# Four small tiles padded: where the tiles of a five-stage transformer program start in SBUF

## The chip, the cores and the metric

The program runs on one core of one Trainium2 chip. The metric is the device time in microseconds of one execution, the median of several runs. The trace is one profiled execution of the same program.

## The reference, cut to what matters

512 tokens of width 1024 pass through two blocks of two layers each. Everything is float32.

```python
for l in range(2):      # first block
    h = rms_norm(x, norm_mix_pre[l])
    proj = h @ w_in[l]                                  # 1024 x 2560
    o_da, o_ret, o_pool = ...   # two-map attention, retention, windowed means
    mix = concatenate([o_da, o_ret, o_pool]) @ w_out[l]
    x = x + rms_norm(mix, norm_mix_post[l])
    h = rms_norm(x, norm_mlp_pre[l])
    u = h @ w_up[l]                                     # 1024 x 5632
    uc = conv_b + sum(conv_w[j] * shifted(u, j) for j in range(3))
    gate, val = split(uc)
    x = x + rms_norm((gelu(gate) * val) @ w_down[l], norm_mlp_post[l])
for l in range(2):      # second block
    x = x + 0.5 * swiglu(rms_norm_2(x), gate, up, down) # inner width 2816
    x = x + hybrid_mixer(rms_norm_2(x))                 # dilated windows, stick breaking, gates
    x = x + 0.5 * swiglu(rms_norm_2(x), gate, up, down)
out = rms_norm_2(x, norm_final)
```

## The kernel before

Ten stages run one after the other: mix1, mlp1, mix1, mlp1 (the first block), then ffn1, mix2, ffn2 twice (the second). In each of them PE does the dense products, and smaller work (attention, retention, pooling, stick breaking) is put between them in program order. That order is fixed when the program is built: every triple of dense matmuls adds a nominal 640 ns to a clock in the program's text (tick, called at the end of each triple), and a generator of small work takes its next step when its credit is positive. No measured time enters into it.

**Weights.** Class Stream loads weights in chunks of 128 x 1024 float32 (tile wraw, DMA from the SP queue), then ACT copies each to whi in float32r (L63), and DVE subtracts to get wlo (L64), so that whi + wlo is the weight. There are 3 wraw and 4 pairs of whi and wlo. Activations are split in the same way: h_hi and h_lo, hid_hi and hid_lo, mix, fm, od and os. A product of two split numbers takes three float32r matmuls: high by high, and the two cross terms.

**Dense products.** Two forms exist. In the feature-major one (fm, fm_block, mm3a: L166, L167, L168) 128 x 128 blocks of the weights are stationary and 512 tokens of h move, eight blocks deep, into a PSUM bank called pa; mix2's two projections use the same three lines with od and os moving, into pp. The opening four chunks of a stage run by halves, 256 tokens each, so that they can begin while the last tokens' norm is still under way. In the token-major form (tm, mm3b: L172, L173, L174) 128 tokens of an activation are stationary and 512 columns (256 for mix2's values) of the weights move, into pb. The activation there is h (mix1's first two products, mix2's values), hid (the down products of mlp1, ffn1 and ffn2), mix (mix1's output) or the split gates fm_hi and fm_lo (mix2's output). For two of mix2's three groups of values the stationary tokens are every fourth one.

**Stage ends.** finish adds the last product to X, squares and scales X for the next norm (xn, L199), and PE transposes the rows (L209) into the next h; the chain of those steps is placed beside the first half matmuls of the next stage.

**Layout.** Tiles lie in pools, in the order in which the pools were opened: const, keep, small, gains, sq, wraw, wparts, then a pool for each stage (phase). A tile takes the bytes of its row in each partition, rounded up to a multiple of 32. const holds ident (512 bytes), mhalf (32 bytes) and X, keep holds h_hi and h_lo, small holds the norms' and the mixers' small tiles and xn. Behind mhalf, X, h_hi, h_lo and xn therefore start 32 bytes past a multiple of 128. gains, wraw, whi, wlo and the stage pools start on a multiple of 128, since what lies in small adds up that way. In mlp1's pool cw (528 bytes, 544 with rounding) and cb (176, 192 with rounding) stand ahead of hid_hi, so hid_hi and hid_lo start at 96 modulo 128; ffn1 and ffn2 use the same function without cw and cb, and hid starts at 0. In mix1's pool cols, share and lam (32, 160 and 32 bytes) put v_da, vg, u, the masks, the tiles fm and the pairs mix_hi, mix_lo at 96. In mix2's pool all tiles start at 0.

Of the kernel before, what the change touches and what calls it, by code (L numbers as in the profile page):

```python
# [11 lines left out]
F32 = mybir.dt.float32  # L12
# [6 lines left out]
L = 2  # L19
D = 1024  # L20
T = 512
NT = T // 128
KD = D // 128
FF = 2816
KF = FF // 128
# [12 lines left out]
class Stream:  # L38
    """Weights in the order of their use: each chunk is loaded, split in two
    float32r parts whose sum it is, and given out."""  # L40

# [42 lines left out]
class Background:  # L84
    """Work that is spread between the dense products: generators, each of which
    yields how much dense work (in ns) it wants before its next step."""

# [4 lines left out]
class Block:  # L92
# [16 lines left out]

# [1 line left out]

# [29 lines left out]

# [1 line left out]

# [31 lines left out]

# [1 line left out]

# [16 lines left out]
    def scaled_rows(self, t, r, gain):  # L194
        """Rows of block t of the norm's output, in two halves."""
        parts = []
        for n in range(2):
            xn = self.small.tile([128, 512], F32, name="xn", bufs=4)
            self.nc.vector.scalar_tensor_tensor(xn, self.X[:, t, n * 512:(n + 1) * 512], r,  # L199
                                                gain[:, n * 512:(n + 1) * 512], op0=OP.mult, op1=OP.mult)  # L200
            parts.append(xn)
        return parts
# [11 lines left out]
    def later(self, ns, t, f):  # L214
        """f, which works on token block t, after so much more dense work."""
        self.pending.append((self.clock + ns, t, f))
        self.pending.sort(key=lambda x: x[0])

    def flush(self, t):
        """Whatever is still to do for the token blocks up to t."""  # L220
        while True:
            i = next((i for i, x in enumerate(self.pending) if x[1] <= t), None)
            if i is None:
                return
            self.pending.pop(i)[2]()

# [1 line left out]

    def fm(self, evacs, halves=False):
        """Feature-major products: one chunk [128, 8, 128] for each of evacs."""  # L230
        tag = self.dense_tag
        blocks = []
        n = self.n_half if halves else 0
        if halves and n < len(evacs):
            self.fm(evacs[:n], True)
            return self.fm(evacs[n:])
        groups = [evacs] if halves else [[e] for e in evacs]
        for group in groups:
            got = []
            for e in group:  # L240
                if not halves:
                    got.append((self.st.take(), self.bank(tag, "pa"), e))
            if halves:
                for h in range(2):
                    self.flush(2 * h + 1)
                    for j, e in enumerate(group):
                        if h == 0:
                            got.append((self.st.take(), self.bank(tag, "pa"), e))
                        (i, w), ps, _ = got[j]
                        c = slice(h * 256, (h + 1) * 256)  # L250
                        self.fm_block(ps, w, c, 256)
                        if h == 1:
                            self.st.release(i)
                            got[j][2](ps)
            else:
                for (i, w), ps, e in got:
                    self.fm_block(ps, w, slice(0, 512), 512)
                    e(ps)
                    self.st.release(i)
# [7 lines left out]
    def tm(self, nk, width, rows, evac, tag, tail=0, opens=False):  # L267
        """Token-major products: nk feature blocks against chunks of CHUNK // width
        blocks of width columns each."""
        per = CHUNK // width  # L270
# [35 lines left out]

# [1 line left out]

    def finish(self, nk, rows, gain, scale=None, post=None, final=False):
        """x += the product of rows with the next weights (scaled, or normed with  # L310
        the gain post), then the next norm's rows on their way to self.H."""
        nc = self.nc
# [62 lines left out]
    def begin(self, gain):  # L375
        """The first norm, in the order in which tokens and weights arrive."""
        nc = self.nc
# [39 lines left out]

# [1 line left out]

# [43 lines left out]
    def mlp1(self, l, next_gain, final):  # L463
        nc, a = self.nc, self.a
        cw = self.phase.tile([128, 3, 2 * KF], F32, name="cw")
        cb = self.phase.tile([128, 2 * KF], F32, name="cb")
        nc.sync.dma_start(cw, a["conv_w"][l])
        nc.sync.dma_start(cb, a["conv_b"][l])
        post = a["norm_mlp_post"][l]
        self.mlp((cw, cb), next_gain, final, post)  # L470
# [3 lines left out]

# [1 line left out]

# [3 lines left out]
    def spare(self, name):  # L480
        """A scratch tile from the slots that the norms use between the stages."""
        return self.small.tile([128, 512], F32, name=name, tag="xn", bufs=4)
# [28 lines left out]

# [1 line left out]

    def mix1(self, l, next_gain, final):
# [10 lines left out]
        load(lams, bass.AP(tensor=s.tensor, offset=s.offset, ap=[[0, 128], [64, 4], [1, 64]]))  # L525
        cols = ph.tile([128, 8], F32, name="cols")
        load(cols, a["mix_cols"][l])
# [80 lines left out]
    def diff_attention(self, fm, v, neglam, gcol, mix):  # L608
# [4 lines left out]
        def scores(h, t):  # L613
            n = 128 * (t + 1)
            q, k = fm[f"q{h}"], fm[f"k{h}"]
            if t == 0:
                rec[h] = self.small.tile([128, NT, 2], F32, name="rec", bufs=3)
            st = self.small.tile([128, 8], F32, name="st")
# [92 lines left out]
    def retention(self, fm, vg, gcols, mix):  # L711
        """The decay of a query and the inverse decay of a key are in their rotary
        tables, so a block's past is one state per head."""
        nc = self.nc
# [74 lines left out]
    def pooling(self, u, share, pw, gcols, mix):  # L789
        """Means over windows of 2 and 4, then 8 and 16 tokens, by halves."""  # L790
        nc = self.nc
# [27 lines left out]

# [1 line left out]

# [101 lines left out]
    @staticmethod  # L923
    def tokens(x, g, t):
        """The tokens of tile t of group g, of x [p, T]: a run of tokens, or the
        tokens that are t modulo 4, one or four whole residue classes."""
        return x[:, t::4] if g else x[:, t * 128:(t + 1) * 128]

    def dilated(self, half, fm, v, o_dil):
# [4 lines left out]
        for s in range(2):  # L934
# [6 lines left out]
            def near(i):  # L941
                """Scores of key blocks 2i and 2i + 1, each for its own and the next block."""
                ps = self.bank(self.bg_tag, "pst")
                for b in (2 * i, 2 * i + 1):
                    n = min(256, T - b * 128)
                    mm(ps[:, (b % 2) * 256:(b % 2) * 256 + n], k[0][:, b * 128:(b + 1) * 128], q[0][:, b * 128:b * 128 + n])
                x = self.scratch("es")
                if i == 0:
                    f = lambda a: a.rearrange("p (a b) -> p a b", a=2)
                    nc.vector.tensor_add(f(x), f(ps), pair)  # L950
                else:
                    nc.vector.tensor_add(x[:, :384], ps[:, :384], self.window_kq3)
                return x
# [49 lines left out]
            yield 900  # L1003
            # weights, numerators and denominators
            mt = m.rearrange("p (i t) -> p t i", t=4)
# [95 lines left out]
def body(ctx, tc, a, out, stages):  # L1101
# [5 lines left out]
    nc.sync.dma_start(B.ident, a["c_ident"])  # L1107
    B.mhalf = B.const.tile([128, 8], F32, name="mhalf")
    nc.vector.memset(B.mhalf, -0.5)
# [13 lines left out]
def constants():  # L1123
    """Tables that depend on the shapes alone."""
    c = {}
# [39 lines left out]
def tiles_a(w):  # L1165
    """[L, D, N] as chunks [L, N // 128, 128, 8 * 128] of whole columns."""
    n = w.shape[2] // 128
    return w.reshape(L, KD, 128, n, 128).transpose(0, 3, 2, 1, 4).reshape(L, n, 128, CHUNK)


def tiles_b(w, width):
    """[L, K, N] as chunks [L, (N // width) * (K // 128 // per), 128, per * width]."""
    per = CHUNK // width
# [4 lines left out]
def arrange(inp):  # L1178
    """The inputs laid out as the program reads them."""
    a = {}  # L1180
# [61 lines left out]
```

## Time and profile before

| | |
|---|---|
| median of 3 runs | 3564.27 us (3563.7 to 3566.45) |
| span of the profiled execution | 3553.4 us |
| PE busy | 3500.0 us, 98% |
| PE weight loads | 2842.4 us, 80% |
| DVE, ACT, POOL busy | 1512.6, 1163.3, 351.3 us |
| DMA | 312 MB, mean 88 GB/s |

The profiled execution's own time is its span of 3553.4 us and what lies around it at the start and the end; the median is 10.9 us above the span. A line of the profile names the program's line, the engine, the operation, out<-in by the tiles' names with buffer numbers left out, the shape and a count. PE's matmuls are pipelined, so their durations overlap: the time that one costs is the distance between two starts.

### The profile page before, as it was taken

How to read it: one execution, taken by the hardware profiler on the slowest of the kernel's cores; microseconds unless marked ns; L12 is line 12 of the kernel's file. 1: busy time of each engine (PE TensorE's matmuls, PEld its weight loads, DVE VectorE, ACT ScalarE, POOL GpSimd, SP SyncE). 2: the span in 40 equal slices, each digit the busy share in tenths (PEclk: the TensorE clock that was granted, in tenths of full speed). 3: DMA queues.
4: the chain of work that ended last, by engine and by line, in shares of the span. 5: the costliest groups of instructions: out<-in, count | busy, mean ns of one | idle time of the engine just before them, and what ended most of it. 6: DMA issues, size and time to landing. Idle time of an engine off the chain costs nothing.

```text
span 3553.4 us, 39868 instructions
## 1 busy us (share of the span) xinstructions
PE 3500.0 (98%) x16304; PEld 2842.4 (80%) x16304; DVE 1512.6 (43%) x1973; ACT 1163.3 (33%) x1854; POOL 351.3 (10%) x412
## 2 busy tenths in 40 slices
PE   8999999999999999999999999999999999999999
PEld 6678887767888788889887888888888988788887
DVE  4655542465554343324543533233332454353322
ACT  4344432334443232222235332222222223532222
POOL 2411100241110000002200100000000220010000
PEclk9999999999999999999999999999999999999999
DMA  4123232312223232222111232323222211123232
GB/s 154 47 73 101 95 107 78 110 48 73 100 95 108 76 102 94 101 101 88 49 60 60 89 102 94 104 86 101 94 100 97 88 48 60 61 90 104 92 104 77
DMA packets 87191, 312.00 MB, mean 88 GB/s; under 512 B 10369, under 2 KB 11073, under 8 KB 87009
## 3 DMA queue, kind: packets, MB, share of 16 engines
q1 hardware_dynamic: 85536, 305.17, 25.3%
q0 software_dynamic: 1472, 4.30, 0.4%
q8 instruction: 128, 2.10, 0.2%
q14 instruction: 55, 0.44, 0.0%
HBM read 307.32 MB, written 2.10 MB: 87 GB/s over the span
## 4 chain that ended last, share of the span: by engine, by line
PE 93%; DVE 3%; ACT 1%; POOL 1%; issue 1%; DMA 0%; DVEq 0%; SPq 0%; POOLq 0%; ACTq 0%
PE pa L166 19%; PE pa L167 18%; PE pa L168 18%; PE pb L172 10%; PE pb L173 10%; PE pb L174 10%; PE pst L932 1%; PE pz L1038 1%; PE psc L625 1%; DVE wlo L64 1%; PE ph L209 1%; PE pod L1026 1%; PE pos L1038 1%; PE po L661 1%; DVE pb L343 0%
## 5 line engine op out<-in xcount | busy, mean ns | idle before, releaser
L64 DVE TENSOR_TENSOR wlo<-wraw,whi 128x1024 fp32r<-128x1024 f32 x556 | 708.5, 1277 | 1207.0 <-ACT whi L63 1205.7
L166 PE MATMUL pa<-h_hi,whi 128*128 128x512 f32 (+1 forms) x3072 | 1180.7, 384 | 4.4 <-ACT h_hi L151 4.4
L167 PE MATMUL pa<-h_lo,whi 128*128 128x512 f32 (+1 forms) x3072 | 1158.6, 377 | 5.7 <-DVE h_lo L152 5.7
L168 PE MATMUL pa<-h_hi,wlo 128*128 128x512 f32 (+1 forms) x3072 | 1157.5, 377 | 0.0
L63 ACT ACTIVATE whi<-wraw 128x1024 fp32r<-128x1024 f32 x556 | 583.3, 1052 | 685.4 <-PE pb L174 516.8
L166 PEld LDWEIGHTS pa<-h_hi,whi 128*128 128x128 f32 x3072 | 578.5, 188 | 136.5 <-issue 16.0
L168 PEld LDWEIGHTS pa<-h_hi,wlo 128*128 128x128 f32 x3072 | 578.3, 188 | 117.8
L167 PEld LDWEIGHTS pa<-h_lo,whi 128*128 128x128 f32 x3072 | 579.0, 188 | 116.2 <-DVE h_lo L152 7.9
L172 PE MATMUL pb<-whi,hid_hi 128*128 128x512 f32 x1056 | 413.8, 392 | 0.0
L174 PE MATMUL pb<-whi,hid_lo 128*128 128x512 f32 x1056 | 413.0, 391 | 0.0
L173 PE MATMUL pb<-wlo,hid_hi 128*128 128x512 f32 x1056 | 413.0, 391 | 0.0
L174 PEld LDWEIGHTS pb<-whi,hid_lo 128*128 128x128 f32 x1056 | 198.1, 188 | 43.7
L173 PEld LDWEIGHTS pb<-wlo,hid_hi 128*128 128x128 f32 x1056 | 198.2, 188 | 43.6
L172 PEld LDWEIGHTS pb<-whi,hid_hi 128*128 128x128 f32 x1056 | 198.2, 188 | 43.0
L426 ACT ACTIVATE hid_hi<-act 128x512 fp32r<-128x512 f32 x88 | 55.7, 633 | 396.8 <-DVE act L437 396.8
L190 POOL TENSOR_TENSOR rs<-ss 128x1 f32<-128x1 f32 x44 | 8.8, 200 | 1635.7 <-ACT sqs L180 1635.7
L437 DVE TENSOR_TENSOR act<-act,pa 128x512 f32<-128x512 f32 x88 | 60.5, 688 | 223.3 <-PE pa L168 223.3
L172 PE MATMUL pb<-whi,h_hi 128*128 128x256 f32 (+1 forms) x384 | 142.3, 371 | 2.7 <-ACT whi L63 2.3
L173 PE MATMUL pb<-wlo,h_hi 128*128 128x256 f32 (+1 forms) x384 | 140.0, 365 | 3.9 <-DVE wlo L64 3.9
L446 DVE SCALAR_TENSOR_TENSOR cv<-pa,cw,cv 128x511 f32<-128x511 f32 (+1 forms) x176 | 131.5, 747 | 27.4 <-ACT cv L444 24.3
L174 PE MATMUL pb<-whi,h_lo 128*128 128x256 f32 (+1 forms) x384 | 139.4, 363 | 0.0
L433 ACT ACTIVATE act<-pa 128x512 f32<-128x512 f32 x88 | 52.5, 597 | 259.4 <-PE pa L168 259.3
(229 smaller groups left out, 3011.1 us busy)
## 6 DMA issues: line engine op xcount, KB each, us to landing
wraw<-w_ffn SPq DMA_DIRECT2D x264, 512.0 KB, 3.2
wraw<-w_mix SPq DMA_DIRECT2D x160, 512.0 KB, 3.2
wraw<-w_mlp SPq DMA_DIRECT2D x132, 512.0 KB, 3.2
X<-x SPq DMA_DIRECT2D x4, 512.0 KB, 7.6
gain<-norm_ffn SPq DMA_DIRECT2D x4, 512.0 KB, 4.1
out<-xn SPq DMA_DIRECT2D x8, 256.0 KB, 2.0
gain<-norm_mix_pre SPq DMA_DIRECT2D x2, 512.0 KB, 5.4
rope_da<-c_rope SPq DMA_DIRECT2D x2, 512.0 KB, 8.8
```

The source lines that it names most:

```text
L63: self.nc.scalar.activation(hi, t, AF.Copy)
L64: self.nc.vector.tensor_sub(lo, t, hi.bitcast(F32))
L166: mm(ps, w[0], h[0], start=first, stop=False)
L167: mm(ps, w[0], h[1], start=False, stop=False)
L168: mm(ps, w[1], h[0], start=False, stop=last)
L172: mm(ps, h[0], w[0], start=first, stop=False)
L173: mm(ps, h[0], w[1], start=False, stop=False)
L174: mm(ps, h[1], w[0], start=False, stop=last)
L426: nc.scalar.activation(hid[0][:, f], h, AF.Copy)
L437: nc.vector.tensor_mul(g, g, ps)
L446: nc.vector.scalar_tensor_tensor(c[:, s:], ps[:, :T - s], cw[:, j, i:i + 1], c[:, s:], op0=OP.mult, op1=OP.add)
L1038: mm = lambda out, lhsT, rhs, first: nc.tensor.matmul(out, lhsT, rhs, start=first, stop=True, skip_group_check=True)
```

## The change

Four small tiles get longer rows; three are cut back to their former size where they are used. mhalf takes 128 bytes in place of 32, so X and everything in const, keep and small behind it moves up by 96 bytes. rec, a small tile of the attention in the pool small, gets a fourth buffer of 32 bytes, so that the pools behind small move up by 96 + 32 = 128. cb takes 224 bytes in place of 192, and cols 64 in place of 32, which moves what follows in the pools of mlp1 and mix1 by another 32. Afterwards X, h, xn, hid, v_da, vg, u, the masks, fm and mix all start on a multiple of 128, and the tiles that did before still do, 128 bytes further up. The order of instructions on every engine and what they wait for stay as they were; the memset of mhalf writes 32 columns in place of 8.

```diff
@@ mlp1
         cw = self.phase.tile([128, 3, 2 * KF], F32, name="cw")
-        cb = self.phase.tile([128, 2 * KF], F32, name="cb")
+        cb = self.phase.tile([128, 2 * KF + 12], F32, name="cb")[:, :2 * KF]
...
@@ mix1
-        cols = ph.tile([128, 8], F32, name="cols")
+        cols = ph.tile([128, 16], F32, name="cols")[:, :8]
...
@@ diff_attention
-                rec[h] = self.small.tile([128, NT, 2], F32, name="rec", bufs=3)
+                rec[h] = self.small.tile([128, NT, 2], F32, name="rec", bufs=4)
...
@@ body
-    B.mhalf = B.const.tile([128, 8], F32, name="mhalf")
+    B.mhalf = B.const.tile([128, 32], F32, name="mhalf")
     nc.vector.memset(B.mhalf, -0.5)
```

The rest of the diff takes out comments and docstrings.

## Rows read from the trace of the kernel before

**Rows 1.** The page: the span, busy time by engine, the chain by line.
```profile
span 3553.4 us, 39868 instructions
...
PE 3500.0 (98%) x16304; PEld 2842.4 (80%) x16304; DVE 1512.6 (43%) x1973; ACT 1163.3 (33%) x1854; POOL 351.3 (10%) x412
...
PE pa L166 19%; PE pa L167 18%; PE pa L168 18%; PE pb L172 10%; PE pb L173 10%; PE pb L174 10%; PE pst L932 1%; PE pz L1038 1%; PE psc L625 1%; DVE wlo L64 1%; PE ph L209 1%; PE pod L1026 1%; PE pos L1038 1%; PE po L661 1%; DVE pb L343 0%
```

**Rows 2.** Timeline of PE, ffn1's up products: start us, duration us, instruction.
```profile
1300.05 0.39 PE L166 MATMUL pa<-h_hi,whi 128*128 128x512 f32 x1
...
1344.85 0.39 PE L166 MATMUL pa<-h_hi,whi 128*128 128x512 f32 x1
```

**Rows 3.** Timeline of PE, mlp1's down product.
```profile
519.72 0.40 PE L173 MATMUL pb<-wlo,hid_hi 128*128 128x512 f32 x1
...
559.86 0.40 PE L174 MATMUL pb<-whi,hid_lo 128*128 128x512 f32 x1
```

**Rows 4.** Timeline of PE, ffn1's down product.
```profile
1509.74 0.39 PE L173 MATMUL pb<-wlo,hid_hi 128*128 128x512 f32 x1
...
1549.86 0.39 PE L173 MATMUL pb<-wlo,hid_hi 128*128 128x512 f32 x1
```

**Rows 5.** Timeline of PE, mix2's projections.
```profile
1956.21 0.39 PE L167 MATMUL pp<-od_lo,whi 128*128 128x512 f32 x1
...
1965.96 0.39 PE L168 MATMUL pp<-os_hi,wlo 128*128 128x512 f32 x1
```

**Rows 6.** Groups by form: count | busy us, mean ns | idle before, releaser.
```profile
L166 PE MATMUL pa<-h_hi,whi 128*128 128x512 f32 x2560 | 1036.0, 405 | 0.0
...
L172 PE MATMUL pb<-whi,hid_hi 128*128 128x512 f32 x1056 | 413.8, 392 | 0.0
...
L166 PE MATMUL pa<-h_hi,whi 128*128 128x256 f32 x512 | 144.8, 283 | 4.4 <-ACT h_hi L151 4.4
...
L172 PE MATMUL pb<-whi,h_hi 128*128 128x256 f32 x256 | 90.0, 352 | 0.0
...
L172 PE MATMUL pb<-whi,mix_hi 128*128 128x512 f32 x128 | 54.2, 424 | 0.0
...
L172 PE MATMUL pb<-whi,h_hi 128*128 128x512 f32 x128 | 52.3, 408 | 2.7 <-ACT whi L63 2.3 <-ACT h_hi L151 0.4
```

**Rows 7.** Timeline of PE, the opening half pieces of ffn1.
```profile
1255.73 0.28 PE L168 MATMUL pa<-h_hi,wlo 128*128 128x256 f32 x1
...
1263.97 0.28 PE L166 MATMUL pa<-h_hi,whi 128*128 128x256 f32 x1
```

**Rows 8.** Timeline of PE, mix2's values: tokens in runs, then every fourth token.
```profile
1650.61 0.28 PE L173 MATMUL pb<-wlo,h_hi 128*128 128x256 f32 x1
...
1655.81 0.28 PE L172 MATMUL pb<-whi,h_hi 128*128 128x256 f32 x1
...
1664.74 0.40 PE L174 MATMUL pb<-whi,h_lo 128*128 128x256 f32 x1
...
1679.91 0.40 PE L173 MATMUL pb<-wlo,h_hi 128*128 128x256 f32 x1
```

**Rows 9.** The tile hid_lo, min/median/max ns: from act (ffn), from cv (mlp1).
```profile
L427 DVE TENSOR_TENSOR hid_lo<-act,hid_hi x88: 691/692/694, 1264.5 to 3427.6; 128x512 fp32r<-128x512 f32 x88
L427 DVE TENSOR_TENSOR hid_lo<-cv,hid_hi x44: 691/693/695, 276.3 to 1116.2; 128x512 fp32r<-128x512 f32 x44
```

**Rows 10.** Windows: length, busy us by engine, granted clock, DMA share, GB/s.
```profile
1266.60:1490.00 223.40, 223.40 (x960) 179.43 (x959) 76.65 (x81) 62.53 (x80) 0.00 (x0) 1.00 0.29 96
...
629.80:633.20 3.40, 3.40 (x12) 3.00 (x13) 3.37 (x4) 0.65 (x1) 0.00 (x0) 0.50 0.62 206
...
2964.60:2967.80 3.20, 3.20 (x16) 2.98 (x16) 0.69 (x1) 0.00 (x0) 0.00 (x0) 0.50 0.47 169
```

**Rows 11.** Waits of PE: waiting line <- releaser: us in total, times, longest us.
```profile
PE ph L209 <- DVE X L345: 7.7, 4, 1.9
...
PE pb L173 <- DVE wlo L64: 3.9, 4, 1.9
```

## The prediction

> **What bounds the kernel now.** I read the page first: PE is busy 98% of a span of 3553.4 us, and six lines of dense products, L166 to L168 and L172 to L174, hold 85% of the chain that ended last [rows 1]. Those lines are the only place where much time can be found, so the question is what one of their matmuls costs and why. The duration column is of no use for that: consecutive matmuls overlap and their ends are modelled. The useful number is the pitch, the distance from one start to the next in a stretch where nothing else runs on PE, and the timeline gives it when the first and the last start are divided by the count between.
>
> In ffn1's up products (weights stationary, h moving) 192 steps take 1344.85 - 1300.05 = 44.80 us, 233.3 ns each [rows 2]. In mlp1's down product (hid stationary, weights moving) 172 steps take 40.14 us, 233.4 ns [rows 3]. In ffn1's down product, which is the same code, 177 steps take 40.12 us: 226.7 ns [rows 4]. In the projections pp of mix2 (weights stationary, od and os moving, the same three lines as ffn1's up products) 43 steps take 9.75 us: 226.7 ns [rows 5]. All four are 512-column matmuls of the same type at a granted clock of 1.00, no wait stands in front of them, and yet there are two pitches, 6.6 ns apart.
>
> What separates the two pairs is the layout. Modulo 128 bytes the weights (whi, wlo) start at 0 everywhere. h starts at 32. hid starts at 96 in mlp1 and at 0 in ffn1 and ffn2, since only mlp1 has cw and cb below it. od and os start at 0. So the pitch is 226.7 where both operands start on a multiple of 128, and 233.3 where either one does not, whether that is the moving one [rows 2, 5] or the stationary one [rows 3, 4]. Code, clock and weights are shared within each pair, which leaves the address and the work of the other engines as candidates.
>
> **The change part by part.** The order of the instructions and their waits is the same on every engine; one memset gets wider. What changes is where tiles lie: X, h, xn, hid in mlp1, and v_da, vg, u, the masks, fm and mix of mix1 move to multiples of 128, and everything that was on one is shifted by exactly 128, so nothing that was aligned loses it.
>
> *512-column products, per matmul 233.3 - 226.7 = 6.6 ns.* Counts come from the groups by form [rows 6]; each row stands for one of three lines. Up products and projections with h moving: 3 x 2560 = 7680, times 6.6 is 50.7 us. Down product of mlp1: two of the six down stages, so a third of 3 x 1056, that is 1056, gives 7.0 us. Output product of mix1 (mix starts at 96): 3 x 128 = 384, 2.5 us. The first two products of mix1, h stationary: another 384, 2.5 us. Sum 62.7 us. The aligned end of each term is a row of this kernel on the same lines, so I take it as it is. In two of these terms no aligned twin of the very product exists (h and mix); there the price is taken from hid, which is stationary in the same lines.
>
> *256-column products with h moving.* The opening four chunks of a stage run by halves: 70 steps take 1263.97 - 1255.73 = 8.24 us, 117.7 ns [rows 7]. The trace has no aligned one of this width. If the cost goes with the columns, an aligned one takes half of 226.7, 113.3, and saves 4.4; if it is a fixed 6.6 per matmul, it saves 6.6; if a half-bank piece is paced by something else, 0. I take 4.4, since 117.7 is itself close to half of 233.3. There are 3 x 512 = 1536 [rows 6]: 6.7 us, between 0 and 10.1.
>
> *256-column products with h stationary (the values of mix2).* There are 3 x 256 = 768 [rows 6]. Half of them read h in runs: 44 steps in 5.20 us, 118.2 ns; by the same reasoning 4.9 x 384 = 1.9 us, between 0 and 2.5. The other half read every fourth token: 65 steps in 15.17 us, 233.4 ns [rows 8], the pitch of a misaligned 512-column one, which fits a stationary read that spans 2048 bytes. I take 6.6 x 384 = 2.5 us, with 0 as the other end.
>
> Gross sum: 62.7 + 6.7 + 1.9 + 2.5 = 73.8 us.
>
> *What the other engines do.* Their price doesn't hang on the address: DVE writes hid_lo in 692 ns where it is aligned and 693 where it isn't [rows 9], so I put nothing on DVE, ACT and POOL. The small fp32 products and the transposes hold under a tenth of the chain [rows 1]; some of their operands move too, I put them at nothing, and leave up to 2 us below for them. The wider memset stands at the start of DVE, beside the first load of x, and rec's fourth buffer only gives back a slot later than before: nothing for either.
>
> *What comes late next.* PE gets 2.9% faster and the engines that feed it do not. In a long dense stretch that is harmless: in ffn1's up products DVE is busy 76.65 of 223.40 us and ACT 62.53 [rows 10]. It matters where PE waits for a chain whose cover is dense work: the residual before the next norm (X, 4 times, 7.7 us) and, in the mixers, the split of weights (wlo, 4 times, 3.9 us) [rows 11]. The cover of such a wait is about 96 half matmuls of 117.7 ns, 11.3 us, and it shrinks by some 0.4 us at each of ten stage ends, at most 4 us; for a split of weights that comes late more often I allow 2 us more. I take 3 of these 6. Net: 73.8 - 3 = 70.8 us.
>
> **The clock.** Nine stretches after the start run at a granted clock of 0.50, of about 3.4 or 6.8 us each and some 44 us together, the first and the last of which are shown [rows 10]. The order of work on PE stays, but everything shifts in time, so a stretch may come or go. At half clock about half of a stretch is lost; three of them more or fewer are some 5 us either way. I take 0.
>
> **The rivals.**
>
> *Only the stationary side pays.* Then h moving is slow for a reason of its own (it is read by PE while ACT and DVE write other tiles, say) and stays at 233.3. The gain is 7.0 + 2.5 + 2.5 + 1.9 + 2.5 = 16.4 us, giving 3548. For it: the one product that runs in two kinds of stage with a change of address is the stationary one [rows 3, 4]. Against it: pp moves aligned tiles through the same lines at 226.7 [rows 5], beside DVE and POOL work of its own. Chance 0.04.
>
> *The address does nothing.* Then the two pitches come from what else runs: mlp1's down product stands after a stage with more DVE and POOL work than ffn1's. The time stays at 3564. Against it: ffn1's up products run at 233.3 while POOL does nothing at all [rows 10], and its down product, a moment later beside the same splitting of weights, at 226.7. Chance 0.04. The Trainium skill's page "SBUF — State Buffer", section "Specifications (TRN2)", would side with this rival: it gives lines of 16 bytes, with a penalty for each crossing, and starts at 32 and 96 are multiples of 16. By that rule the sum would be zero; the trace doesn't agree, with two pitches for starts that the rule treats alike.
>
> *The denser stream costs clock.* If PE, with fewer stalls in the array's stream, were granted 0.50 more often, each us of it would cost about half a us. To eat the 70.8 us takes 142 us more at half clock, and to end 7 us slower 156 us: from 44 to about 200 us, giving 3571 or more. Against it: the stretches that already run at 226.7 have 1.00 throughout, among them the 120 us of ffn1's down product. Chance 0.02.
>
> **How the numbers follow.** The profiled span is 3553.4 us; the median of the runs is 3564.27, 10.9 us more, which lie around the span and stay. Forecast: 3564.3 - 70.8 = 3493.5, say 3494, chance 0.90. Its low end: all the 256-column terms at 6.6 (10.1 + 2.5 + 2.5), no new waits, 2 us of small products and two or three half-clock stretches fewer, 62.7 + 15.1 + 2 + 4 = 83.8, 3480 (3480.5). Its high end: nothing from the 256-column terms, 6 us of waits, 5 us of clock, 62.7 - 11 = 51.7, 3512. The rivals lie outside and hold 0.10 together, so the range 3480 to 3512 leaves out no more than 2 in 10. Faster by over 0.2% (7 us, about what a measurement of this kernel can tell from no change): forecast and first rival, 0.94. Within 0.2%: 0.04. Slower: 0.02.
>
> **What would show it.** After the change the pitch in ffn1's up products should be 226.7, in mlp1's down product too, with ffn1's down product unchanged. If the up products stay at 233.3 and mlp1's down product falls, the first rival holds; if neither moves, the second. The opening pieces of 256 columns should come at 113 ns and the strided ones of mix2 at 227. Idle time of PE should grow by a few us at the ends of stages, in front of the transposes and the split of h. The prediction is wrong if aligned h and aligned weights meet at another pitch than od and os do, or if new waits of PE add up to more than 6 us.

## The result

The changed kernel takes 3510.27 us, median of four runs (3506.64 to 3511.65), against 3565.36 us before (four runs by then, 3563.7 to 3566.86). The ratio is 0.9841, with a 95% interval of 0.9827 to 0.9855: 1.6% or 55 us faster. The forecast was 3494 within 3480 to 3512, so direction and range held and the gain was 16 us smaller than forecast, 55 where 71 were expected. The reason given for it turned out to be half right, as the experiments show.

### The profile page after: what moved, and what is told of

It is laid out like the page before. It is cut to its first block, busy times and chain, and to the rows that moved or that the text cites. A ratio compares the mean times of both kernels' runs of the same rounds, so it can differ in the third digit from the quotient of the medians.

```text
span 3508.7 us, 39868 instructions
## 1 busy us (share of the span) xinstructions
PE 3456.3 (99%) x16304; PEld 2855.7 (81%) x16304; DVE 1510.2 (43%) x1973; ACT 1161.9 (33%) x1854; POOL 350.6 (10%) x412
## 4 chain that ended last, share of the span: by engine, by line
PE 92%; DVE 4%; ACT 1%; POOL 1%; issue 1%; DMA 0%; DVEq 0%; SPq 0%; POOLq 0%; ACTq 0%
PE pa L166 18%; PE pa L167 18%; PE pa L168 18%; PE pb L172 10%; PE pb L173 10%; PE pb L174 10%; PE pst L932 1%; PE pz L1038 1%; PE psc L625 1%; DVE wlo L64 1%; PE ph L209 1%; PE pod L1026 1%; PE pos L1038 1%; DVE pb L343 0%; PE po L661 0%
## 5 line engine op out<-in xcount | busy, mean ns | idle before, releaser
L166 PE MATMUL pa<-h_hi,whi 128*128 128x512 f32 (+1 forms) x3072 | 1170.6, 381 | 4.6 <-ACT h_hi L151 4.6
L167 PE MATMUL pa<-h_lo,whi 128*128 128x512 f32 (+1 forms) x3072 | 1147.6, 374 | 5.7 <-DVE h_lo L152 5.7
L168 PE MATMUL pa<-h_hi,wlo 128*128 128x512 f32 (+1 forms) x3072 | 1145.9, 373 | 0.0
L166 PEld LDWEIGHTS pa<-h_hi,whi 128*128 128x128 f32 x3072 | 581.8, 189 | 121.8 <-issue 16.2
L168 PEld LDWEIGHTS pa<-h_hi,wlo 128*128 128x128 f32 x3072 | 581.4, 189 | 102.6
L167 PEld LDWEIGHTS pa<-h_lo,whi 128*128 128x128 f32 x3072 | 582.5, 190 | 100.9 <-DVE h_lo L152 7.9
L172 PE MATMUL pb<-whi,hid_hi 128*128 128x512 f32 x1056 | 413.1, 391 | 0.0
L174 PE MATMUL pb<-whi,hid_lo 128*128 128x512 f32 x1056 | 412.1, 390 | 0.0
L173 PE MATMUL pb<-wlo,hid_hi 128*128 128x512 f32 x1056 | 411.9, 390 | 0.0
L174 PEld LDWEIGHTS pb<-whi,hid_lo 128*128 128x128 f32 x1056 | 198.8, 188 | 41.6
L173 PEld LDWEIGHTS pb<-wlo,hid_hi 128*128 128x128 f32 x1056 | 199.1, 189 | 41.1
L172 PEld LDWEIGHTS pb<-whi,hid_hi 128*128 128x128 f32 x1056 | 199.1, 189 | 41.1
L172 PE MATMUL pb<-whi,h_hi 128*128 128x256 f32 (+1 forms) x384 | 141.7, 369 | 2.3 <-ACT whi L63 2.0
L173 PE MATMUL pb<-wlo,h_hi 128*128 128x256 f32 (+1 forms) x384 | 139.1, 362 | 3.9 <-DVE wlo L64 3.9
L174 PE MATMUL pb<-whi,h_lo 128*128 128x256 f32 (+1 forms) x384 | 138.3, 360 | 0.0
```

The costliest lines, as they stand in the source:

```text
L166: mm(ps, w[0], h[0], start=first, stop=False)
L167: mm(ps, w[0], h[1], start=False, stop=False)
L168: mm(ps, w[1], h[0], start=False, stop=last)
L172: mm(ps, h[0], w[0], start=first, stop=False)
L173: mm(ps, h[0], w[1], start=False, stop=False)
L174: mm(ps, h[1], w[0], start=False, stop=last)
```

## The profile after, beside the one before

The page of the changed kernel: span, busy time, chain by line, beside [rows 1].

```profile
span 3508.7 us, 39868 instructions
...
PE 3456.3 (99%) x16304; PEld 2855.7 (81%) x16304; DVE 1510.2 (43%) x1973; ACT 1161.9 (33%) x1854; POOL 350.6 (10%) x412
...
PE pa L166 18%; PE pa L167 18%; PE pa L168 18%; PE pb L172 10%; PE pb L173 10%; PE pb L174 10%; PE pst L932 1%; PE pz L1038 1%; PE psc L625 1%; DVE wlo L64 1%; PE ph L209 1%; PE pod L1026 1%; PE pos L1038 1%; DVE pb L343 0%; PE po L661 0%
```

PE lost 43.7 us of busy time; DVE, ACT and POOL lost 0.7 to 2.4 us, PE's weight loads gained 13.3 us, and the chain hangs on the same lines. Timeline of PE in the changed kernel: ffn1's up products, mlp1's down product, ffn1's down product, ffn1's opening half pieces, and mix2's values with tokens in runs and with every fourth token (first and last start of each stretch).

```profile
1299.73 0.39 PE L168 MATMUL pa<-h_hi,wlo 128*128 128x512 f32 x1
...
1342.80 0.39 PE L166 MATMUL pa<-h_hi,whi 128*128 128x512 f32 x1
...
499.72 0.39 PE L172 MATMUL pb<-whi,hid_hi 128*128 128x512 f32 x1
...
539.84 0.39 PE L172 MATMUL pb<-whi,hid_hi 128*128 128x512 f32 x1
...
1499.65 0.39 PE L174 MATMUL pb<-whi,hid_lo 128*128 128x512 f32 x1
...
1539.78 0.39 PE L174 MATMUL pb<-whi,hid_lo 128*128 128x512 f32 x1
...
1238.73 0.28 PE L168 MATMUL pa<-h_hi,wlo 128*128 128x256 f32 x1
...
1246.89 0.28 PE L167 MATMUL pa<-h_lo,whi 128*128 128x256 f32 x1
...
1627.26 0.28 PE L172 MATMUL pb<-whi,h_hi 128*128 128x256 f32 x1
...
1632.90 0.28 PE L174 MATMUL pb<-whi,h_lo 128*128 128x256 f32 x1
...
1640.82 0.40 PE L172 MATMUL pb<-whi,h_hi 128*128 128x256 f32 x1
...
1655.98 0.40 PE L174 MATMUL pb<-whi,h_lo 128*128 128x256 f32 x1
```

In order: 190 steps in 43.07 us are 226.7 ns, where [rows 2] had 233.3. 177 steps in 40.12 us are 226.7, where [rows 3] had 233.4. ffn1's down product stays at 226.7, 177 steps in 40.13 us, as in [rows 4]. So far as forecast. Then the surprises: 68 steps in 8.16 us are 120.0 ns where [rows 7] had 117.7, and 47 steps in 5.64 us are 120.0 where [rows 8] had 118.2: the 256-column pieces became slower. And 65 steps in 15.16 us are 233.2 ns: the strided products of [rows 8] did not move at all.

## The experiments

All spans and clocks quoted are those of the profiled execution of the kernel named, all ratios are to the kernel before, run beside it.

**Everything at 32, everything at 64.** In the traces so far a tile that is off a multiple of 128 always meets weights that are on one. Two theories fit: each operand's own start counts, or the difference between the two. A wider mhalf on top of the change moves all dense tiles, weights too, by the same 32 bytes (40 columns, below) or 64 (48 columns).

```diff
-    B.mhalf = B.const.tile([128, 32], F32, name="mhalf")
+    B.mhalf = B.const.tile([128, 40], F32, name="mhalf")
```

> All dense tiles start at 32 modulo 128, weights too, so both operands of every product are off a multiple of 128 and at the same phase. Theory A (each operand's own start counts): no 512-column product keeps a pitch of 226.7 ns; it is 233.3 if one misfit is paid once, or 240 if both are paid; 13,344 products' worth of 512 columns at 233.3 give some 25 us over the kernel before, 3590 us, at 240 some 3670. Theory B (the two operands' starts must agree modulo 128, wherever they are): 226.7 ns everywhere, 3510 us as after the change.

> The same with all dense tiles at 64 modulo 128. Theory A with a unit of 128 bytes: as with 32, 233.3 or 240 ns per 512-column product and 3590 to 3670 us. Theory A with a unit of 64 bytes: 226.7 ns and 3510 us. Theory B: 226.7 ns and 3510 us too, so this run speaks on the unit only if the run at 32 is slow.

Measured: 3510.63 us (ratio 0.985, 0.9834 to 0.9867) and 3514.43 us (0.9859, 0.9844 to 0.9874). Timeline of PE, ffn1's up products, everything at 32:

```profile
1299.72 0.39 PE L168 MATMUL pa<-h_hi,wlo 128*128 128x512 f32 x1
...
1342.79 0.39 PE L166 MATMUL pa<-h_hi,whi 128*128 128x512 f32 x1
```

190 steps in 43.07 us, 226.7 ns, the same as after the change, with not one dense tile on a multiple of 128. With everything at 64 the same products come at 226.7 ns as well. The theory that each start counts by itself is out. What counts is how the starts of the two operands differ.

**One half of the change, then the other.** The paddings of cb and cols alone (hid and mix move), and those of mhalf and rec alone (X, h and xn move; rec's rows keep their length, it gets a fourth buffer).

```diff
 stat_only: the kernel before with
+        cb = self.phase.tile([128, 2 * KF + 12], F32, name="cb")[:, :2 * KF]
+        cols = ph.tile([128, 16], F32, name="cols")[:, :8]
 move_only: the kernel before with
+    B.mhalf = B.const.tile([128, 32], F32, name="mhalf")
+                rec[h] = self.small.tile([128, NT, 2], F32, name="rec", bufs=4)
```

> Only cb and cols padded: the stationary tiles hid and mix move to a multiple of 128, h stays at 32. By the prices of the trace (1056 products with hid, 384 with mix, 6.6 ns each) 9.5 us less than the kernel before, 3556 us; the up products stay at 233.3 ns, mlp1's down product falls to 226.7. If the stationary side did nothing: 3565.

> Only mhalf and rec padded: h, X and xn move to a multiple of 128, hid in mlp1 and mix stay at 96. If the terms add up, this keeps the change's gain of 55 us less the 9.5 us of the other part: about 3520 us, up products at 226.7, mlp1's down product at 233.3, the opening pieces of 256 columns at 120 ns as after the change (117.7 before).

Measured: 3557.96 us (0.9978, 0.9969 to 0.9988) and 3523.34 us (0.988, 0.9866 to 0.9895), against 3565.89 before. The parts give 7.9 and 42.6 us, 50.5 together against 55.1 for the change, which the intervals of 3 to 5 us either way allow. Timeline of PE, ffn1's up products with the first part alone:

```profile
1299.20 0.39 PE L167 MATMUL pa<-h_lo,whi 128*128 128x512 f32 x1
...
1342.14 0.39 PE L168 MATMUL pa<-h_hi,wlo 128*128 128x512 f32 x1
```

The same of mlp1's down product with the second part alone:

```profile
519.68 0.39 PE L173 MATMUL pb<-wlo,hid_hi 128*128 128x512 f32 x1
...
559.81 0.39 PE L174 MATMUL pb<-whi,hid_lo 128*128 128x512 f32 x1
```

With the first part alone the up products keep 233.3 ns (184 steps in 42.94 us), with the second alone mlp1's down product does (172 steps in 40.13 us); over all steps, mlp1's down product comes at 226.8 with the first part, the up products at 227.2 with the second. So the stationary and the moving side both pay, and the first rival of the prediction is out.

**How exactly must the starts agree?** h is moved against the weights by 64, 16 and 128 bytes; the weights, hid, mix, od and os keep agreeing with each other modulo 256. (At 64, h lies 64 bytes short of agreement, as hid in mlp1 lay 32 short of it in the kernel before; at 16 it lies past it. Which tile is on the multiple of 256 itself doesn't matter, by the run with everything at 32.)

```diff
 rel64:  mhalf [128, 48], rec bufs=6
 rel128: mhalf [128, 64], rec bufs=8
 rel16:
+        self.H = tuple(self.keep.tile([128, KD * T + 64], F32R, name=n)[:, 4:4 + KD * T].rearrange(...)
+                       for n in ("h_hi", "h_lo"))
```

> X, h and xn start at 64 modulo 128, weights, hid, mix, od and os at 0. The runs with everything at 32 and at 64 kept 226.7 ns, so what counts is how the starts of the two operands differ. If they must agree modulo 128, products with h come at 233.3 ns and the time is near 3565 less 9.5 (the part of hid and mix), 3556 us; if modulo 64, they keep 226.7 and the time is 3510 us. A difference of 64 may also cost more than one of 32: 240 ns would give some 3610 us.

> h starts 16 bytes past a multiple of 128, weights and all else on one. If a difference of any size costs the same, products with h come at 233.3 ns and the time is 3556 us; if the price goes with the difference, half of it, some 3535 us; if 16 bytes are below what counts, 3510 us.

> h starts 128 bytes past a multiple of 256, weights on a multiple of 256. If agreement modulo 128 is enough, 226.7 ns and 3510 us as after the change; if the unit is 256 bytes or more, products with h come at 233.3 ns or above and the time is 3556 us or more.

Measured: 3550.33 us (0.9952, 0.9937 to 0.9967), 3544.39 us (0.993, 0.9914 to 0.9947) and 3550.04 us (0.9953, 0.9938 to 0.9967). Timeline of PE, ffn1's up products, at a difference of 64:

```profile
1299.73 0.40 PE L167 MATMUL pa<-h_lo,whi 128*128 128x512 f32 x1
...
1342.90 0.39 PE L166 MATMUL pa<-h_hi,whi 128*128 128x512 f32 x1
```

The same at a difference of 16:

```profile
1299.78 0.39 PE L166 MATMUL pa<-h_hi,whi 128*128 128x512 f32 x1
...
1342.86 0.40 PE L166 MATMUL pa<-h_hi,whi 128*128 128x512 f32 x1
```

The same at a difference of 128:

```profile
1299.74 0.40 PE L168 MATMUL pa<-h_hi,wlo 128*128 128x512 f32 x1
...
1342.91 0.39 PE L167 MATMUL pa<-h_lo,whi 128*128 128x512 f32 x1
```

Timeline of PE, ffn1's opening half pieces, at a difference of 64:

```profile
1253.81 0.28 PE L168 MATMUL pa<-h_hi,wlo 128*128 128x256 f32 x1
...
1261.97 0.28 PE L168 MATMUL pa<-h_hi,wlo 128*128 128x256 f32 x1
```

At 64, 185 steps in 43.17 us: 233.3 ns. At 16, 186 steps in 43.08 us: 231.6. At 128, 185 steps in 43.17 us: 233.3, with both operands on multiples of 128. That last one refutes the change's own rule: two tiles on multiples of 128 can be as slow as before, if one is on a multiple of 256 and the other isn't. In the changed kernel all weights, h, hid, mix, od and os happen to agree modulo 256. A difference of 256 costs nothing: in the changed kernel hid differs from whi by 256 modulo 512 in mlp1 and by 0 in ffn1, and both down products take 226.7 ns. The prices at 64, 16 and 128 above are those with h moving. With h stationary (mix1's first two products, mean of all steps within a product under 260 ns) they are not all the same: 227.0 ns in agreement, 229.0 at 16, 229.2 at 64, 232.8 at 128 and 233.3 at 32. The last stretch shows the 256-column pieces at their best, 72 steps in 8.16 us or 113.3 ns (another stretch of the same stage has 117.8), at a difference that is bad for the 512-column ones.

**The kernel before, profiled once more**, without any edit.

> The kernel before, profiled once more. Its first profiled execution had a span 10.9 us below the median of the runs, the changed kernel's one only 1.6 below. If the 10.9 us lie around the span, this span is 3553 again. If the first profiled execution was a short one (fewer stretches at half clock, 44 us of them), this span is about 3563, with some 20 us more at half clock.

Span and mean granted clock of the first profiled execution of the kernel before:

```profile
core 0: 3553.4 us, clock 0.993
```

The same of the second profiled execution of the kernel before:

```profile
core 0: 3563.2 us, clock 0.990
```

The same of the changed kernel:

```profile
core 0: 3508.7 us, clock 0.991
```

The second execution took 3565.07 us in all, 1.9 more than its span, and the profiled run of the changed kernel (3510.61) stands 1.9 above its span too. So about 2 us lie around the span, not 10.9. A mean clock of 0.993 means that some 1.4% of the span, 50 us, was at half clock, and 0.990 means 2%, 71 us; 21 us more at half clock are some 10 us of time. The first trace of before was a short execution.

**One part in three, one chunk in four.** On top of the change, wlo alone at 32 modulo 256; then the same for every fourth chunk only; then h_lo alone at 32.

```diff
 wlo32:
+            lo = self.split_pool.tile([128, CHUNK + 64], F32R, name="wlo")[:, 8:8 + CHUNK]
 wlo32_quarter:
+            o = 8 if self.split % 4 == 0 else 0
+            lo = self.split_pool.tile([128, CHUNK + 64], F32R, name="wlo")[:, o:o + CHUNK]
 hlo32: h_lo = a tile of KD * T + 64 columns, from its 9th on
```

> As after the change, but wlo alone starts at 32 modulo 256, all else on a multiple of 256. Where weights are stationary, wlo is loaded for L168 only. If a matmul's pitch is set by its moving tile against its own stationary tile, L168 takes 233.3 ns and L166 and L167 keep 226.7. If it is set by the moving tile against the next matmul's stationary tile, which is loaded meanwhile, L167 takes 233.3 and the other two keep 226.7. If the two can't be told apart by line, all three share the loss. In each case one of three is slow: a third of some 13,000 times 6.6 ns, 28 us over the changed kernel, about 3538 us.

> As the run with wlo at 32, but for every fourth chunk of the weights only; the other three chunks have wlo on a multiple of 256. There all three lines lost, though one of three meets another phase. If the loss stays with the 24 matmuls of the chunk, every fourth chunk takes 24 times 233.3 ns, the others 24 times 226.7, and the time is 3510 plus a quarter of 72, 3528 us. If one misfit slows what comes after it for long, more chunks are slow: up to 3582 us.

> As after the change, but h_lo alone starts at 32 modulo 256; h_hi, the weights and all else on a multiple of 256. In the up products one of three matmuls (L167) moves h_lo. If one misfit among three costs all three, as with wlo, the up products come at 233.3 ns on average and the time is some 3556 us; if it costs its own 6.6 ns alone, 228.9 ns and 3525 us.

Measured: 3582.59 us (1.0053, 1.0038 to 1.0068), 3529.14 us (0.9899, 0.987 to 0.9928) and 3550.8 us (0.9962, 0.9946 to 0.9978). Timeline of PE, ffn1's up products, with wlo at 32 throughout:

```profile
1299.75 0.39 PE L168 MATMUL pa<-h_hi,wlo 128*128 128x512 f32 x1
...
1342.91 0.40 PE L167 MATMUL pa<-h_lo,whi 128*128 128x512 f32 x1
```

Two matmuls out of that stretch, and the load of the second one's weights (PEld), which runs beside the first:

```profile
1310.71 0.40 PE L167 MATMUL pa<-h_lo,whi 128*128 128x512 f32 x1
...
1310.95 0.39 PE L168 MATMUL pa<-h_hi,wlo 128*128 128x512 f32 x1
...
1310.71 0.19 PEld L168 LDWEIGHTS pa<-h_hi,wlo 128*128 128x128 f32 x1
```

The same with wlo at 32 in one chunk of four: the start of every 24th matmul, which is one chunk (lines are one higher in that kernel).

```profile
1299.76 0.40 PE L168 MATMUL pa<-h_lo,whi 128*128 128x512 f32 x1
...
1305.35 0.39 PE L168 MATMUL pa<-h_lo,whi 128*128 128x512 f32 x1
...
1310.80 0.39 PE L168 MATMUL pa<-h_lo,whi 128*128 128x512 f32 x1
...
1316.24 0.39 PE L168 MATMUL pa<-h_lo,whi 128*128 128x512 f32 x1
...
1321.68 0.40 PE L168 MATMUL pa<-h_lo,whi 128*128 128x512 f32 x1
...
1327.27 0.39 PE L168 MATMUL pa<-h_lo,whi 128*128 128x512 f32 x1
```

ffn1's up products with h_lo at 32:

```profile
1299.84 0.40 PE L167 MATMUL pa<-h_lo,whi 128*128 128x512 f32 x1
...
1343.06 0.39 PE L168 MATMUL pa<-h_hi,wlo 128*128 128x512 f32 x1
```

With wlo at 32 throughout, 185 steps in 43.16 us are 233.3 ns on average, though two of three matmuls have operands in agreement; worked out line by line from all starts, the usual distance to the next start is 232 or 233 ns after L166, 239 after L167 and 228 after L168. One misfit in three costs as much as three, 20 ns per triple, and most of it falls on the two matmuls ahead of the misfit's own. My expectation of 3538 us was wrong by that: the whole stream paid. It pays only as long as the misfit recurs: in the quarter run a chunk takes 5.59 us every fourth time (233 ns a matmul) and 5.44 to 5.45 in between (227), and the time is 1 us over the expected 3528. With h_lo as the odd one the up products come at 231.1 ns (187 steps, 43.22 us), also far above the 228.9 of a loss that stays with its own matmul; the time, 3551 us, lies nearer to the 3556 of a full loss than to 3525.

On the partner (own stationary tile, or the next one, loaded meanwhile) the traces lean one way. The load of wlo for L168 starts with L167 and takes 188 ns, no longer than in the changed kernel, and the longest distance, 239 ns, is the one after L167, not the one after L168 (228). It is the same where h_lo is the odd stationary tile, in mix1's first two products of the last run: 232 ns after L172, 239 after L173, which runs while h_lo is loaded, and 229 after L174, which uses it. Where the odd tile moves, the longest distance follows its own matmul: 236 ns after L173 in the down products with wlo at 32, 236 after L167 in the up products with h_lo at 32. All four fit the next tile as the partner, and the first two don't fit the own one. But the loss spreads over the neighbours too, which neither theory says, so this is not settled.

**The strided values.** The strided products kept 233 ns at any start. On top of the change, the values of the two strided groups are computed for tokens in runs and put in place by 64 small transfers.

```diff
-                return [self.tokens(x[:, k], g, t) for x in self.H]
+                return [self.tokens(x[:, k], 0, t) for x in self.H]
...
+                x = self.scratch("vx")[:, :384].rearrange("p (a c d) -> p a c d", a=2, c=3)
+                nc.gpsimd.memset(x[:, :, 1], 1.0)
+                nc.scalar.activation(x[:, :, 0::2], src, AF.Copy)
+                for r in range(NT):
+                    nc.scalar.dma_start(v[32 * t:32 * t + 32, r, 2 * g:2 * g + 2], x[r::4])
```

> As after the change, but the values of mix2's two strided groups are computed for tokens in runs (h stationary without a stride) and put in their places by small transfers from ACT's queue. The strided products kept 233 ns for 256 columns after the change, whatever the start of h; if the stride of the stationary read is what they pay for, 384 of them fall to 121 ns, 43 us less: 3467 us. If they are slow for another reason, 3510 us or, with the transfers late, more.

Measured: 3483.35 us, ratio 0.9775 (0.9759 to 0.9791), 27 us below the changed kernel and the fastest of all, but 16 us above the 3467 expected. Windows of the changed kernel over the value products and the stretch behind them (length, busy us of PE, PEld, DVE, ACT, POOL, granted clock, DMA share, GB/s):

```profile
1625.00:1681.30 56.30, 56.30 (x290) 56.26 (x289) 9.34 (x9) 10.35 (x17) 3.89 (x3) 1.00 0.16 52
1681.40:1781.30 99.90, 99.16 (x454) 79.42 (x453) 57.40 (x85) 23.01 (x33) 20.58 (x12) 0.93 0.17 59
```

The same two windows of the kernel with the values in runs:

```profile
1630.00:1664.50 34.50, 34.50 (x289) 34.49 (x288) 8.10 (x8) 8.87 (x16) 4.95 (x11) 1.00 0.34 114
1664.60:1767.00 102.40, 98.94 (x455) 78.81 (x453) 58.55 (x86) 24.26 (x35) 20.58 (x12) 0.95 0.18 62
```

Its waits of PE, the one that the changed kernel's list doesn't have (us in total, times, longest), and its span and clock:

```profile
PE pm L974 <- DVE es L968: 6.5, 2, 3.8
```

```profile
core 0: 3478.3 us, clock 0.988
```

The value products take 34.5 us in place of 56.3, 21.8 less in each of two stages: the 43 us expected are there, so the stride of the stationary read was the price. The weight loads show it as well, at 1645 us of the changed kernel for every fourth token and at 1310 us for a tile in runs:

```profile
1645.12 0.33 PEld L173 LDWEIGHTS pb<-wlo,h_hi 128*128 128x128 f32 x1
...
1310.16 0.19 PEld L167 LDWEIGHTS pa<-h_lo,whi 128*128 128x128 f32 x1
```

Then 2.5 us in the first stage, and 3.9 in the second, come back in the stretch behind, where PE now waits for a score tile (6.5 us in two waits that the changed kernel doesn't have among its longer ones). The rest of the difference between 43.6 and 30.4 us (the spans) is of the size of the clock: 0.988 against 0.991 is some 20 us more at half clock, 10 us of time. It is not the chance of one execution: all four of this kernel have a mean clock of 0.987 or 0.988, the four of the changed kernel 0.991 to 0.993, the seven of the kernel before that ran beside this one 0.990 or 0.991. What in this kernel brings it on was not tested.

## Why the prediction was right, and where it was not

**The 512-column term held in size.** Forecast 62.7 us. Worked out from all steps under 260 ns within a product, the mean pitch fell from 233.3 to 227.1 with h moving (7680 matmuls, 47.2 us), from 233.3 to 226.8 in mlp1's down product (1056, 6.9 us), from 233.3 to 227.0 in mix1's first two products and from 233.2 to 227.8 in its output product (384 each, 2.4 and 2.1 us): 58.6 us. It is 4 us below the forecast because in stretches with small products between them the dense ones settle at 228 to 231 and not at 226.7.

**The 256-column terms had the wrong sign.** This is the step that failed most: "if the cost goes with the columns, an aligned one takes half of 226.7". It doesn't. In agreement, 226.7 ns at 2.4 GHz (the granted clock is 1.00 in these stretches) are 544 cycles for 512 columns and 120.0 ns are 288 for 256: 32 more than the columns in both. Out of agreement by 32 bytes, 233.3 ns are 48 cycles more, but 117.7 only 26. Over all steps under 140 ns the mean rose from 116.8 to 119.9 in the half pieces (1536 matmuls, 4.7 us) and from 118.2 to 119.6 in mix2's values in runs (384, 0.5 us), a loss of 5.2 us where a gain of 8.6 was expected; the bound of 0 for these terms excluded a loss without a reason. The strided products gave 0 and not 2.5 us: their price is the stride of the stationary read, not its start, as the last experiment shows. Together these terms are 16 us off, as much as the whole miss; the 4 us of the first term are about made up for by the 3 us of waits that did not come.

**The waits** did not grow, where 3 us were subtracted for them and PE was to idle a few us more. Waits of PE in the changed kernel:

```profile
PE ph L209 <- DVE X L345: 7.7, 4, 1.9
...
PE pb L173 <- DVE wlo L64: 3.9, 4, 1.9
```

Both are as in [rows 11], and PE's idle time, span less busy time, is 52.4 us after 53.4.

**The 10.9 us around the span** were not there. They were half-clock time that the profiled execution of before happened to miss, so the difference of the first two spans (44.7 us) understates the gain; against the second execution it is 54.5 us, near the 55.1 of the medians. The prediction subtracted its sum from the median, so this did no harm to the forecast. The accounting against that second execution: 58.6 - 5.2 = 53.4 us from the pitches, the rest of 1.1 us from clock and waits together.

**The reason was half right.** The prediction read from four stretches that a product is fast "where both operands start on a multiple of 128". All four fit that, and also a condition which I did not list as a rival: that the two operands agree in phase. In the kernel before, the weights sit at one phase throughout, so being off a multiple and being out of step with the partner were the same thing. The runs with everything at 32 and with h 128 bytes off separate them: agreement modulo 256 is what counts for the 512-column products, and the change works because its shift brings all partners to it. That the rows before the change pointed to multiples of 128, and that the change built on them brought agreement modulo 256 as well, was luck: the run at 128 satisfies the prediction's rule and keeps 233.3 ns. The rival that the address does nothing is out. The clock rival is out for this change: its mean clock of 0.991 lies between those of the two executions of before. A loss of clock does stand in the run with the values in runs, from a cause that is not shown. The 16-byte lines of the Trainium skill's page "SBUF — State Buffer", section "Specifications (TRN2)", do not forecast this case: a difference of 16 bytes, one such line, already costs 5 ns.

## What to carry to other kernels

Where float32r products run back to back on PE, compare pitches of the same lines in different stages and look where the operands lie relative to each other; padding a few small tiles until stationary and moving tiles agree modulo 256 bytes was worth 1.6% here, 58.6 us on the 512-column products less 5.2 us that the 256-column ones lost by it. So weigh the shares of the widths first. Before a cause is read from a natural comparison, list what else is common to the fast cases: one run that shifts everything by the same amount tells an absolute rule from a relative one. And a stationary read with a stride can cost more than moving the result into place afterwards.

## What the runs showed of the hardware that was not expected

- The pitch of a 512-column float32r matmul in a stream depends on the difference of its operands' starts. With h moving it is 226.7 ns in agreement, 231.6 at 16 bytes, 233.3 at 32, 64 and 128; with h stationary 227.0, 229.0, 233.3, 229.2 and 232.8. A difference of 256 (hid in mlp1) costs nothing.
- At 256 columns the order turns: with h moving 120.0 ns at 0, 118.7 at 16, 117.7 at 32, 113.3 to 117.8 at 64, 118.6 at 128.
- One misfit in a triple of matmuls costs the whole triple (233.3 ns on average with wlo, 231.1 with h_lo), and the loss is gone in the next chunk without one.
- A stationary operand that takes every fourth element keeps a 256-column matmul at 233 ns, where one in runs allows 120; its load takes 330 ns in place of 188.
- Two executions of one program differed by 10 us, which is what their times at half clock make up (0.993 against 0.990, some 21 us). The kernel with the values in runs had 0.987 or 0.988 in each of four executions.

Why agreement of the two starts helps is not shown by any run; that the load of the next weights goes on during a matmul is in the trace (PEld is busy 81% of the span beside PE; the lines with wlo at 32 above), and that its read and the moving one meet in SBUF is no more than a guess.
